# A two-layer decoder trunk on one core: three moves in the order of transposes, loads and sums

## The chip, the core and the metric

The kernel runs on one core of a Trainium2 chip. The metric is the time of one execution on the device in microseconds (us). Lower is better. The engines are TensorE (PE in the profile; PEld is its loading of weights), VectorE (DVE), ScalarE (ACT), GpSimd (POOL) and SyncE (SP), which issues nearly all DMAs in one queue.

## What is computed

The input x has 512 rows of 1024 float32 values. Two layers follow, each a token mixer and a gated MLP, every one ahead of a plain residual add. The first mixer is a gated DeltaNet, the second an attention with a sliding window whose keys and values are projected once. Cut to what the change touches:

```python
def gated_deltanet(hn, w_in, conv_w, a_log, dt_bias, out_norm_w, w_out):
    proj = hn @ w_in                      # q, k, v, z, b, a
    ...
    beta = sigmoid(b)
    g = -exp(a_log) * softplus(a + dt_bias)
    o = chunked_gated_delta_rule(q, k, v, g, beta)   # triangular inverse per chunk, then a scan over chunks
    o = rmsnorm(o, out_norm_w) * silu(z)
    return o.reshape(bsz, t, GDN_V_DIM) @ w_out

def shared_kv(h, kv_norm_w, w_kv):
    kv = rmsnorm(h, kv_norm_w) @ w_kv
    k, v = jnp.split(kv, 2, axis=-1)
```

The trunk is x + gated_deltanet, + conv_gated_mlp, then shared_kv, + sliding_window_sink_attention, + conv_gated_mlp, and a last rmsnorm.

## The kernel before

**Products in three passes.** Every large product is made of float32r matmuls of 128 x 512 in three passes (mm3): the high part of the weights by the high part of the data (L145), by its low part (L146), and the low part of the weights by the high part of the data (L147). Data lie with features on the partitions and the 512 tokens along the row, in pieces xh and xl of 128 features. A load of 1 MB brings 256 columns of a weight matrix into `stage` (two buffers). `cast` makes of each half of it a tile whi on ScalarE (L129) and a tile wlo on VectorE (L130), three buffers each. A product sums eight pieces, so 24 matmuls, into a PSUM bank. There are three banks d, two g, two s and one p.

**What sets the order.** Each engine works through its own list in order. A scheduler builds the lists from the program's text, from priorities and from its own costs. In the DeltaNet part a table of words (ORDER, with SHIFT) gives the priorities: key, query and value projections, z projections of the output gates ("z"), the inverses ("I"), their blocks ("L"), the scan ("C"), the gates ("g"). So whatever moves one step can move many others. SP's queue is one such list. A DMA that waits there holds back all that follow.

**The first part.** x is normalized and transposed, then the first key projection and the 48 gate columns are multiplied. The gate chain (L285 to L301) runs over ScalarE and VectorE: sigmoid, softplus, a scan over each chunk (L289) and the differences R (L292). R is transposed by L324 into a g bank and copied into `gt`, of which ngc, egc, egd and egl are made. `columns` (L185 to L196) loads a table of per-channel numbers into an `acc` row (L189), transposes it through a g bank (L192) and copies it out (L194). The MLP's conv table fcw comes in two such pieces. The key norms transpose kT (L385), also through g.

**The inverse and the scan.** For each group of four heads, `solve` (L511, L517) inverts the 32-wide diagonal blocks on VectorE. The result goes to DRAM (td, L520) and comes back as four loads into Xg (L523). `levels` then joins the blocks for each of two pairs of heads, in four dependent steps on PE: L541/L542 into s, copied to pz by ScalarE (L543, L544); L548 to L550 into s, negated by VectorE into Xg and sy (L552 to L554); L561 into p, copied to p6s by ScalarE (L564); L568 into s, subtracted by VectorE from sy (L571). After that come the four chunks of the scan: L588 with the state S, L603 with sy into s, copied to us (L607), L611 for the next state (L617), L628 for the output (L631). Between such dependent steps stand products of projections, which keep PE at work.

**Gates and residual.** `gate` loads a head's output (L667) and its z (L668), scales it by f_c, the output norms, on ScalarE (L671), transposes it (L674), multiplies it (L675) and stores it as yd (L676). The output projection loads yd back (L766), splits each row in a high and a low part (L150, L151) and makes mm3 products of it. YROLE names the buffers: heads 12 and 13 are ktok, 14 and 15 are vt. The residual is x transposed: for each of eight pieces a load into an `acc` row (role hsq, L777), four transposes into g (L780), a copy into h (L781).

**Keys and values.** `attention` normalizes h into kxh and kxl, calls `rstd_rows` and then loops over keys (kv = 0) and values (kv = 1), each with a load of 1 MB and two products. `rstd_rows` sums squares on ScalarE and VectorE (L797, L801), multiplies by ones (L804), takes the root (L806, L807), spreads it (L816, L823) and copies it (L825); the products are scaled by it (L1118), and keys are split into kbh and kbl (L1125 to L1128). The queries follow. Ahead of the attention lies the first MLP, `ffn(0, hT)`, whose last down products (L990 to L992) go straight over into the key products on PE.

Of the kernel before, what the change touches and what calls it, by code (L numbers as in the profile page):

```python
# [17 lines left out]
P = 128  # L18
T = 512
# [22 lines left out]
def kernel(  # L42
# [34 lines left out]
    def nm(s):  # L77
        cnt[0] += 1
        return f"{s}_{cnt[0]}"
# [30 lines left out]
    def bank(tag):  # L110
        return psum.tile([P, T], F32, tag=tag, bufs=BANKS[tag], name=nm(tag))

    def const(shape, dt=F32, s="c"):
        return cp.tile(list(shape), dt, name=nm(s))


    def load_stage(w, r0, kt, c0):
        st = wpool.tile([P, 8, 256], F32, tag="stage", bufs=2, name=nm("stage"))
        SP.dma_start(st[:, :kt, :], tiles_of(w, r0, kt, c0))
        return st  # L120
# [4 lines left out]
    def cast(st, kt, half, m=P):  # L125
        hi = wpool.tile([P, 8, P], F32R, tag="whi", bufs=3, name=nm("whi"))
        lo = wpool.tile([P, 8, P], F32R, tag="wlo", bufs=3, name=nm("wlo"))
        src = st[:, :kt, half * P : half * P + m]
        S.copy(hi[:, :kt, :m], src)  # L129
        V.tensor_tensor(lo[:, :kt, :m], src, hi[:, :kt, :m].bitcast(F32), op=ALU.subtract)  # L130
        return hi, lo

    def weights():
        return [wpool.tile([P, 8, P], F32R, tag=t, bufs=3, name=nm(t)) for t in ("whi", "wlo")]
# [184 lines left out]
    mnegr = const([P, P], F32R, s="mnegr")  # L319
    S.copy(mnegr[:], mneg[:])  # L320

    gtp = bank("g")
    for c in range(NC):
        PE.transpose(gtp[:, c * 80 : c * 80 + 80], R[0:80, c * P : (c + 1) * P], ident[0:80, 0:80])  # L324
    gt = const([P, NC, 80], s="gt")
    S.copy(gt[:], gtp[:, 0 : NC * 80].rearrange("p (c r) -> p c r", c=NC))

    def hc(ap):
        return ap.rearrange("p c h -> p h c")

    beta_t, gc_t, gd_t = hc(gt[:, :, 0:16]), hc(gt[:, :, 32:48]), hc(gt[:, :, 64:80])
    ngc = const([P, 16, NC], s="ngc")
    V.tensor_scalar(ngc[:], gc_t, -1.0, None, op0=ALU.mult)
    egc = const([P, 16, NC], s="egc")
    S.activation(egc[:], gc_t, AF.Exp)
    negegc = const([P, 16, NC], s="negegc")
    V.tensor_scalar(negegc[:], egc[:], -1.0, None, op0=ALU.mult)
    egd = const([P, 16, NC], s="egd")
    S.activation(egd[:], gd_t, AF.Exp)
    gl16 = const([P, 16, NC], s="gl16")  # L340
    V.tensor_tensor(gl16[:], gc_t, gd_t, op=ALU.add)
    egl = const([P, 16, NC], s="egl")
    S.activation(egl[:], gl16[:], AF.Exp)

    Xg = main.tile([P, 4, T], F32, tag="Xg", bufs=1, name="Xg")
    G.memset(Xg[:], 0.0)
# [407 lines left out]
    def r2(role, dt=F32):  # L754
        return row(nxt(role, ROLES[role]), dt)

    def wide(role):
        return pair(nxt("wide", YROLE), F32R)


    yh, yl = [], []
    for h2 in range(HV // 2):
# [8 lines left out]
    h22 = [pair("pz") for _ in range(2)]  # L771
    hT = [h4[:, m, :] for m in range(4)] + [h22[m // 2][:, m % 2, :] for m in range(4)]
    h_pairs = [h4[:, 0:2, :], h4[:, 2:4, :], h22[0][:], h22[1][:]]
    for m in range(KD):
        xr = r2("hsq")
        x3 = xr[:].rearrange("p (c e) -> p c e", c=NC)
        SP.dma_start(x3, x[0, :, m * P : (m + 1) * P].rearrange("(c p) e -> p c e", p=P))  # L777
        pt = bank("g")
        for c in range(NC):
            PE.transpose(pt[:, c * P : (c + 1) * P], x3[:, c, :], ident[:])  # L780
        S.copy(hT[m], pt[:])  # L781
# [11 lines left out]
    def rstd_cols(h):  # L793
# [16 lines left out]
    def third_stage():  # L810
        return main.tile([P, 6, 256], F32, tag="st3", bufs=1, name=nm("st3"))

    def rstd_rows(h):
        rt = rstd_cols(h)
# [287 lines left out]
    def attention(h):  # L1102
# [5 lines left out]
                G.memset(t[0:64, 1, :].bitcast(F32), 0.0)  # L1108
                G.memset(t[64:128, 0, :].bitcast(F32), 0.0)
        kxh, kxl = normed(h, NKV)  # L1110
        rs = rstd_rows(h)
        for kv in range(2):
            st = load_stage(w_kv, 0, 8, 256 * kv)
            for i in range(2):
                ps = bank("d")
                mm3(ps[:], cast(st, 8, i), KD, kxh, kxl)
                f = r2("va")
                V.tensor_tensor(f[:], ps[:], rs[:], op=ALU.mult)  # L1118
                if kv == 0:
                    for j in range(2):  # L1120
                        g = 2 * i + j
                        src = f[64 * j : 64 * j + 64, :]
                        near, far = (slice(0, 64), slice(64, 128)) if j == 0 else (slice(64, 128), slice(0, 64))
                        hn_, hf_ = kbh[g][near, j, :], kbh[g][far, 1 - j, :]
                        S.copy(hn_, src)  # L1125
                        S.copy(hf_, src)
                        V.tensor_tensor(kbl[g][near, j, :], src, hn_.bitcast(F32), op=ALU.subtract)
                        V.tensor_tensor(kbl[g][far, 1 - j, :], src, hn_.bitcast(F32), op=ALU.subtract)  # L1128
                else:
                    pt = bank("g")  # L1130
                    for c in range(NC):
                        PE.transpose(pt[:, c * P : (c + 1) * P], f[:, c * P : (c + 1) * P], ident[:])
                    S.copy(Vp[:, :, i * P : (i + 1) * P], pt[:].rearrange("p (c e) -> p c e", c=NC))
# [84 lines left out]
                V.tensor_tensor(h[m], h[m], ps[:], op=ALU.add)  # L1218

    ffn(0, hT)  # L1220
    attention(hT)
    ffn(1, hT, last=True)

# [52 lines left out]
```

## Time and profile before

| what | value |
|---|---|
| median of 3 runs | 1440.92 us (1440.52 to 1442.91) |
| the profiled execution | 1439.8 us, its span 1438.0, so 1.8 us lie outside the span |
| mean granted TensorE clock | 0.996 |
| PE idle in the span | 36.6 us, 8.2 of them while the first piece of x comes in |

The span is what the profiler saw from the first to the last instruction. A row of a timeline has the start, the duration, engine, line, operation, out<-in, the tile's size and, in brackets, how long the engine stood idle before it and whom it waited for. In a row of SP the duration is that of the issue, or, with a count, the stretch that several issues take. A row of waits has the total, the number and the longest. Matmuls of 128 x 512 show a duration of 0.39 us but start 0.23 us apart, because they are pipelined.

### The profile page before, as it was taken

To read this page: it belongs to the slowest core of one execution; us is meant where nothing else is said; L and a number is where in the kernel's file an instruction comes from. 1 tells how busy PE (TensorE), PEld (TensorE's weight loads), DVE (VectorE), ACT (ScalarE), POOL (GpSimd) and SP (SyncE) were. 2 spreads that over 40 slices of the span, in tenths; PEclk is the share of its full clock that TensorE was granted. 3 is DMA by queue.
4 is the path that set the end of the run, shared out by engine and by line. 5 is a ranking of instruction groups with operands and counts; after the bars stand their busy time and mean duration, and the time that the engine had idled before them with its cause. 6 is when DMAs were issued, how large, how long until landed. Compare 5 with 4: busy or idle time off the path is not lost.

```text
span 1438.0 us, 21635 instructions
## 1 busy us (share of the span) xinstructions
PE 1401.4 (97%) x8266; PEld 1165.2 (81%) x8266; DVE 1120.6 (78%) x2056; ACT 770.8 (54%) x1518; POOL 20.0 (1%) x47
## 2 busy tenths in 40 slices
PE   7999999999999999999999999999999999999998
PEld 5777878878876888888988888777788888988887
DVE  5896887979764538889968889787757888977896
ACT  7764666666555434444335445588745444344443
POOL 1000000000000000000000002000000000000000
PEclk9999999999999999999999999999999999999999
DMA  5334254264367323321333223311132322332222
GB/s 156 88 106 114 78 174 121 76 182 125 103 220 227 125 88 110 104 74 53 123 124 111 74 81 111 111 59 45 59 108 90 118 81 66 112 123 88 96 70 77
DMA packets 163084, 152.85 MB, mean 106 GB/s; under 512 B 24164, under 2 KB 150693, under 8 KB 162981
## 3 DMA queue, kind: packets, MB, share of 16 engines
q1 hardware_dynamic: 160722, 151.27, 33.3%
q8 instruction: 65, 1.06, 0.3%
q10 hardware_dynamic: 2259, 0.20, 0.2%
q14 instruction: 38, 0.31, 0.1%
HBM read 134.65 MB, written 16.80 MB: 105 GB/s over the span
## 4 chain that ended last, share of the span: by engine, by line
PE 83%; DVE 8%; DMA 6%; ACT 2%; issue 1%; SPq 0%; DVEq 0%; ACTq 0%
PE d L145 21%; PE d L147 20%; PE d L146 20%; DVE wlo L130 2%; PE s L588 1%; PE p L1191 1%; DMA ol<-od 1%; PE d L992 1%; PE g L1186 1%; PE s L603 1%; PE s L628 1%; PE d L990 1%; PE s L992 1%; PE d L991 1%; DMA stage<-in_a_w_in_dram 1%
## 5 line engine op out<-in xcount | busy, mean ns | idle before, releaser
L145 PE MATMUL d<-xh,whi 128*128 128x512 f32 x1192 | 475.2, 400 | 2.9 <-ACT whi L129 2.8
L146 PE MATMUL d<-xl,whi 128*128 128x512 f32 x1192 | 472.8, 398 | 0.0
L147 PE MATMUL d<-xh,wlo 128*128 128x512 f32 x1192 | 472.0, 398 | 0.7 <-DVE wlo L130 0.7
L129 ACT CAST whi<-stage 128x1024 fp32r<-128x1024 f32 (+2 forms) x236 | 229.1, 976 | 230.3 <-PE d L146 153.9
L130 DVE TENSOR_TENSOR wlo<-stage,whi 128x1024 fp32r<-128x1024 f32 (+2 forms) x236 | 265.5, 1129 | 69.2 <-ACT whi L129 68.6
L145 PEld LDWEIGHTS d<-xh,whi 128*128 128x128 f32 x1192 | 224.6, 188 | 51.2 <-ACT whi L129 3.4
L147 PEld LDWEIGHTS d<-xh,wlo 128*128 128x128 f32 x1192 | 224.3, 188 | 51.5 <-DVE wlo L130 2.1
L146 PEld LDWEIGHTS d<-xl,whi 128*128 128x128 f32 x1192 | 224.3, 188 | 46.2 <-issue 1.0
L237 DVE SCALAR_TENSOR_TENSOR acc<-d,cwc,acc 128x511 f32<-128x511 f32 (+2 forms) x96 | 70.7, 739 | 8.3 <-ACT acc L234 7.9
L851 DVE TENSOR_TENSOR sz<-d,p6s 128x512 f32<-128x512 f32 x58 | 39.9, 689 | 40.9 <-PE d L147 38.4
L873 ACT ACTIVATE dt<-dt 128x512 f32<-128x512 f32 x44 | 27.8, 632 | 81.7 <-DVE dt L856 81.7
L856 DVE SCALAR_TENSOR_TENSOR va<-sz,fcw,va 128x511 f32<-128x511 f32 (+1 forms) x58 | 43.4, 747 | 1.8 <-ACT va L854 0.9
L856 DVE SCALAR_TENSOR_TENSOR dt<-sz,fcw,dt 128x511 f32<-128x511 f32 (+1 forms) x58 | 43.3, 746 | 0.9
L511 DVE TENSOR_TENSOR p6s<-sN,sT 64x31 f32<-64x31 f32 (+15 forms) x124 | 40.7, 328 | 2.5 <-DMA sN<-nd 0.5
L517 DVE TENSOR_TENSOR sT<-sT,p6s 64x31 f32<-64x31 f32 (+15 forms) x124 | 41.0, 330 | 1.9
L129 ACT CAST whi<-st 128x768 fp32r<-128x768 f32 (+1 forms) x30 | 23.7, 791 | 30.5 <-DMA st<-in_ffn_w_down_dram 5.6
L851 DVE TENSOR_TENSOR zl<-d,p6s 128x512 f32<-128x512 f32 x30 | 20.7, 689 | 24.0 <-PE d L147 23.3
L636 ACT ACTIVATE rq<-o 128x128 f32<-128x128 f32 x64 | 19.0, 298 | 28.4 <-DVE o L631 15.8
L1174 ACT ACTIVATE dt<-dt,sm 128x256 f32<-128x256 f32 (+1 forms) x64 | 30.3, 474 | 6.7 <-DVE sm L1170 6.6
L875 DVE TENSOR_TENSOR va<-dt,va 128x512 f32<-128x512 f32 x44 | 30.4, 691 | 1.2
L130 DVE TENSOR_TENSOR wlo<-st,whi 128x768 fp32r<-128x768 f32 (+1 forms) x30 | 26.8, 898 | 1.9 <-ACT whi L129 1.8
L854 ACT ACTIVATE dt<-sz,normc,fcw 128x512 f32<-128x512 f32 x29 | 23.7, 817 | 5.2 <-DVE sz L851 5.1
(745 smaller groups left out, 2796.5 us busy)
## 6 DMA issues: line engine op xcount, KB each, us to landing
stage<-in_ffn_w_up_dram SPq DMA_DIRECT2D x44, 1024.0 KB, 5.2
stage<-in_a_w_in_dram SPq DMA_DIRECT2D x23, 1024.0 KB, 5.8
stage<-in_ffn_w_down_dram SPq DMA_DIRECT2D x16, 768.0 KB, 4.7
stage<-in_a_w_out_dram SPq DMA_DIRECT2D x8, 1024.0 KB, 5.5
st<-in_ffn_w_down_dram SPq DMA_DIRECT2D x8, 768.0 KB, 5.8
zd<-sz SPq DMA_DIRECT2D x16, 256.0 KB, 2.0
od<-o SPq DMA_DIRECT2D x16, 256.0 KB, 2.5
stage<-in_b_w_q_dram SPq DMA_DIRECT2D x4, 1024.0 KB, 5.0
```

The lines of the kernel that those rows point to most:

```text
L129: S.copy(hi[:, :kt, :m], src)
L130: V.tensor_tensor(lo[:, :kt, :m], src, hi[:, :kt, :m].bitcast(F32), op=ALU.subtract)
L145: PE.matmul(ps, hi[:, k, :m], xh[k], start=first and k == 0, stop=False)
L146: PE.matmul(ps, hi[:, k, :m], xl[k][:], start=False, stop=False)
L147: PE.matmul(ps, lo[:, k, :m], xh[k], start=False, stop=last and k == kt - 1)
L237: V.scalar_tensor_tensor(acc[:, d:], ps[:, : T - d], col, acc[:, d:], op0=ALU.mult, op1=ALU.add)
L511: V.tensor_tensor(tv, N[:, s, s + 1 : 32].unsqueeze(2).to_broadcast([64, n, m]), Tm[:, s : s + 1, 0:m].to_broadcast([64, n, m]), op=ALU.mult,)
L517: V.tensor_tensor(Tm[:, s + 1 : 32, 0:m], Tm[:, s + 1 : 32, 0:m], tv, op=ALU.subtract)
L851: V.tensor_tensor(u[:], ps[:], rs[:], op=ALU.mult)
L856: V.scalar_tensor_tensor(acc[:, d:], u[:, : T - d], tap(2 - d, t), acc[:, d:], op0=ALU.mult, op1=ALU.add)
L875: V.tensor_tensor(b[:], a[:], b[:], op=ALU.mult)
L1174: S.activation(e3[:, j, :], e3[:, j, :], AF.Exp, bias=ngm[:, j : j + 1], accum_out=den[:, j : j + 1])
```

## The change

It has three parts. The first wraps the gates' transposes and the six steps made of them in `tc.high_priority(-112000)`, which lowers their place in the table's order by 112 words. The second gives the residual's eight pieces of x rows of their own: three `f` rows, three pieces of the 6 x 256 buffer st3, and two more `f` rows. Six small GpSimd copies of f_c's column of head 8 into these rows set the time from which they may be filled. The third loads the key weights of w_kv into three `f` rows and the `gr` row after the first MLP's text (`load_rows`), where they are free in that MLP's second half, casts them from there in pieces of 128 x 256 (`cast_rows`), loads only the values through `stage`, and puts `rstd_rows` behind the keys' two products. New lines shift the numbers: L145 is L158 after, L192 is L205, L324 is L342, L385 is L400, L541 to L571 are L556 to L586, L603 is L618, L667 is L682, L777 and L780 are L801 and L804.

```diff
+    def load_rows(w, tags):
+        rows = [row(t)[:].rearrange("p (k c) -> p k c", k=2) for t in tags]
+        for i, r in enumerate(rows):
+            SP.dma_start(r, tiles_of(w, 2 * i * P, 2, 0))
+        return rows
+
+    def cast_rows(rows, half):
+        w = weights()
+        for i, r in enumerate(rows):
+            cast_to(w, 2 * i, r[:, :, half * P : half * P + P])
+        return w
...
-    gtp = bank("g")
-    for c in range(NC):
-        PE.transpose(gtp[:, c * 80 : c * 80 + 80], R[0:80, c * P : (c + 1) * P], ident[0:80, 0:80])
-    gt = const([P, NC, 80], s="gt")
...
+    with tc.high_priority(-1000 * 112):
+        gtp = bank("g")
+        for c in range(NC):
+            PE.transpose(gtp[:, c * 80 : c * 80 + 80], R[0:80, c * P : (c + 1) * P], ident[0:80, 0:80])
+        gt = const([P, NC, 80], s="gt")
...
+    x6 = third_stage()[:].rearrange("p k c -> p (k c)")
+    xrows = [row("f")[:] for _ in range(3)] + [x6[:, T * u : T * u + T] for u in range(3)]
+    for xr in xrows:
+        G.tensor_copy(xr[:, 0:1], f_c[:, 8, 0:1])
+    xrows += [row("f")[:] for _ in range(2)]
     for m in range(KD):
-        xr = r2("hsq")
-        x3 = xr[:].rearrange("p (c e) -> p c e", c=NC)
+        x3 = xrows[m].rearrange("p (c e) -> p c e", c=NC)
...
-        rs = rstd_rows(h)
         for kv in range(2):
-            st = load_stage(w_kv, 0, 8, 256 * kv)
+            if kv == 1:
+                st = load_stage(w_kv, 0, 8, 256 * kv)
+            products = []
             for i in range(2):
                 ps = bank("d")
-                mm3(ps[:], cast(st, 8, i), KD, kxh, kxl)
+                mm3(ps[:], cast(st, 8, i) if kv else cast_rows(key_weights, i), KD, kxh, kxl)
+                products.append(ps)
+
+            if kv == 0:
+                rs = rstd_rows(h)
+            for i, ps in enumerate(products):
                 f = r2("va")
...
     ffn(0, hT)
+    key_weights = load_rows(w_kv, ("f", "f", "f", "gr"))
     attention(hT)
```

The scheduler builds new lists from this. Three places follow, as the lists give them. The first is PE's list around the gates, before and after: d_121 and d_131 are products of key and query projections, g_69 is the gates' bank, g_88, g_91 and g_94 are those of `columns`, g_103 the key norms'. Before:

```order
L146 MATMUL d_121_541<-xl_45_196,whi_122_542 128x512
L324 MATMUL g_69_322<-ident_6_80,sz_60_280 128x80
L192 MATMUL g_88_363<-ident_6_80,acc_87_358 128x17
L147 MATMUL d_121_541<-xh_44_195,wlo_123_543 128x512
L324 MATMUL g_69_322<-ident_6_80,sz_60_280 128x80 x2
L145 MATMUL d_131_632<-xh_23_132,whi_132_633 128x512
L324 MATMUL g_69_322<-ident_6_80,sz_60_280 128x80
L192 MATMUL g_91_369<-ident_6_80,acc_90_367 128x128
```

After:

```order
L160 MATMUL d_131_632<-xh_44_195,wlo_133_634 128x512
L342 MATMUL g_69_322<-ident_6_80,sz_60_280 128x80
L205 MATMUL g_88_363<-ident_6_80,acc_87_358 128x17
L342 MATMUL g_69_322<-ident_6_80,sz_60_280 128x80 x3
L205 MATMUL g_91_369<-ident_6_80,acc_90_367 128x128
L205 MATMUL g_94_375<-ident_6_80,acc_93_373 128x128
L400 MATMUL g_103_418<-kT_49_205 128x128 x4
L158 MATMUL d_135_667<-xh_23_132,whi_136_668 128x512
```

The gates moved behind all 24 products of d_131, and the columns' transposes with them. Before, fourteen matmuls stand between g_91's transpose and g_94's; after, none does.

The second is SP's queue when the last group's inverse comes back from DRAM (td to Xg), with the gates' loads (ol, zl), z's stores (zd) and gate stores (yd). Before:

```order
L520 DMA td_354<-sT_549_3446 64x1024
L523 DMA Xg_341<-td_354 32x16x32 x2
L676 DMA yd_357<-zl_624_4072 128x512
L667 DMA ol_626_4086<-od_355 128x4x128
L523 DMA Xg_341<-td_354 32x16x32
L668 DMA zl_627_4087<-zd_356 128x512
L523 DMA Xg_341<-td_354 32x16x32
L667 DMA ol_629_4101<-od_355 128x4x128
```

After (the six loads of x by L801 stand some rows ahead of it):

```order
L675 DMA zd_356<-sz_674_4319 128x512
L538 DMA Xg_341<-td_354 32x16x32
L683 DMA zl_627_4087<-zd_356 128x512
L683 DMA va_676_4323<-zd_356 128x512
L682 DMA ol_629_4101<-od_355 128x4x128
L538 DMA Xg_341<-td_354 32x16x32
L691 DMA yd_357<-zl_627_4087 128x512
L538 DMA Xg_341<-td_354 32x16x32
L682 DMA ol_632_4116<-od_355 128x4x128
L683 DMA zl_630_4102<-zd_356 128x512
L538 DMA Xg_341<-td_354 32x16x32
```

The second to fourth loads of Xg moved behind the loads of gates 9 to 11 and the store of gate 9.

The third is PE's list at the same group's second pair of heads: s_620 is its second step, p_621 and s_622 the third and fourth, s_635 the first product of the scan, d_687 a z projection. Before:

```order
L550 MATMUL s_620_4020<-sy_618_3999,pz_78_344 32x32
L146 MATMUL d_687_4403<-xl_27_142,whi_688_4404 128x512
L147 MATMUL d_687_4403<-xh_26_141,wlo_689_4405 128x512
L145 MATMUL d_687_4403<-xh_29_150,whi_688_4404 128x512
L561 MATMUL p_621_4048<-Xg_341,nt_543_3416 64x64 x8
L146 MATMUL d_687_4403<-xl_30_151,whi_688_4404 128x512
L147 MATMUL d_687_4403<-xh_29_150,wlo_689_4405 128x512
L145 MATMUL d_687_4403<-xh_32_159,whi_688_4404 128x512
L568 MATMUL s_622_4059<-sy_618_3999,p6s_79_345 64x64 x8
L603 MATMUL s_635_4131<-vt_589_3771,sy_613_3927 128x128 x2
```

After:

```order
L565 MATMUL s_620_4020<-sy_618_3999,pz_78_344 32x32
L576 MATMUL p_621_4048<-Xg_341,nt_543_3416 64x64 x8
L583 MATMUL s_622_4059<-sy_618_3999,p6s_79_345 64x64
L618 MATMUL s_635_4131<-vt_589_3771,sy_613_3927 128x128
L583 MATMUL s_622_4059<-sy_618_3999,p6s_79_345 64x64 x7
L618 MATMUL s_635_4131<-vt_589_3771,sy_613_3927 128x128
```

The z products between the steps moved ahead of the whole pair; the last of them stand between the second and third step of the first pair (s_615 and p_616).

More of the change, by code (lines that the diff above doesn't have):

```diff
@@ L758, in wide, with third_stage @@
         return pair(nxt("wide", YROLE), F32R)
+    def third_stage():
+        return main.tile([P, 6, 256], F32, tag="st3", bufs=1, name=nm("st3"))
     yh, yl = [], []
@@ L808, in rstd_cols @@
         return rt
-    def third_stage():
-        return main.tile([P, 6, 256], F32, tag="st3", bufs=1, name=nm("st3"))
     def rstd_rows(h):
```

28 lines of the change are left out of this document (14 added, 14 removed).

## The prediction

> **What bounds the kernel now.** I read the page first, then TensorE's waits, then the granted clock of the stretches around the longest waits. The page's second line gives the bound:
>
> ```profile
> PE 1401.4 (97%) x8266; PEld 1165.2 (81%) x8266; DVE 1120.6 (78%) x2056; ACT 770.8 (54%) x1518; POOL 20.0 (1%) x47
> ```
>
> TensorE is busy 1401.4 us, 97% of the span, so only the 3% in which it isn't, and what the clock loses behind them, can be won. The waits say where they lie (line, what was waited for, total, times, longest):
>
> ```profile
> PE d L145 <- ACT whi L129: 2.8, 1, 2.8
> PE g L324 <- DVE sz L292: 2.4, 1, 2.4
> ...
> PE g L780 <- DMA acc<-in_x_dram: 1.6, 3, 0.7
> ...
> PE s L588 <- DVE S L617: 1.0, 1, 1.0
> PE g L385 <- ACT kT L238: 0.9, 1, 0.9
> PE g L780 <- DVE va L675: 0.8, 1, 0.8
> ...
> PE g L1132 <- DVE va L1118: 0.7, 1, 0.7
> ```
>
> The change aims at five of them: L324 (the gates), both of L780 (the residual), L145 with its 2.8 and L1132 (keys and values). The stretches (busy us of PE, PEld, DVE, ACT and POOL, then the granted clock) show what follows a long wait:
>
> ```profile
> 37.00:40.00 3.00, 0.57 (x4) 0.18 (x2) 2.90 (x10) 0.66 (x2) 0.00 (x0) 1.00 0.44 93
> 40.00:44.00 4.00, 4.00 (x14) 3.17 (x14) 2.70 (x6) 3.93 (x5) 0.00 (x0) 0.57 0.63 213
> 400.00:420.00 20.00, 20.00 (x256) 15.99 (x254) 9.23 (x19) 9.75 (x28) 0.61 (x2) 1.00 0.60 197
> 890.00:897.00 7.00, 4.23 (x31) 3.71 (x30) 7.00 (x13) 4.91 (x6) 6.50 (x13) 1.00 0.45 151
> 897.00:905.00 8.00, 7.79 (x29) 5.82 (x28) 6.25 (x8) 3.42 (x6) 0.18 (x1) 0.79 0.40 132
> ```
>
> After 2.4 us without work the clock is 0.57 for 4 us, which loses 4 x 0.43 = 1.7 us more; after 2.8 us it is 0.79 for 8 us (8 x 0.21 = 1.7). The row 400 to 420 is full: that stretch has nothing to win, and it matters below.
>
> **Part A, the gates.** The rows around the wait (start, duration, engine, line; behind them a load and its time from issue to landing):
>
> ```profile
> 36.70 0.39 PE L145 MATMUL d<-xh,whi 128*128 128x512 f32 x1
> 36.93 0.40 PE L146 MATMUL d<-xl,whi 128*128 128x512 f32 x1
> 39.75 0.26 PE L324 MATMUL g<-ident,sz 80*128 80x80 f32 x1 [2.43 <-DVE sz L292]
> ...
> 43.77 0.42 PE L145 MATMUL d<-xh,whi 128*128 128x512 f32 x1
> ```
> ```profile
> 37.43 0.37 SPq L119 DMA_DIRECT2D stage<-in_a_w_in_dram  x1
> 40.22 0.34 SPq L189 DMA_DIRECT2D acc<-in_ffn_conv_w_dram  x1
> ```
> ```profile
> acc<-in_ffn_conv_w_dram SPq DMA_DIRECT2D x1, 64.0 KB, 2.9
> ```
> ```profile
> stage<-in_a_w_in_dram SPq DMA_DIRECT2D x23, 1024.0 KB, 5.8
> ```
>
> A product starts 0.23 us behind the one ahead of it. From 37.16 (36.93 + 0.23) to 43.77, 6.6 us, PE did some 2.4 us of work, seven products and six small transposes: the gates' place costs 4.2 us now. In the new order 25 products run there, so PE is at the gates at 37.16 + 25 x 0.23 = 42.9, when the VectorE chain (done at 39.75) has long ended: that wait goes.
>
> But the columns' transposes and the key norms (L385, now L400) keep their turn behind the gates on the two g banks, so they move too, and with them a load. The second conv table (acc_93) takes the row of acc_87, which is free only when g_88 is transposed, after the gates: about 43.4, not 40.2. SP's queue now has the next 1 MB of weights (stage_215) just ahead of it, which needs only wlo_146 and is issued at about 43. Behind the gates PE has one more transpose (g_91) and then stands at g_94 with everything queued behind it, all products of the next key and query projections included. If the table lands 2.9 us after its issue as before, at 46.3, the wait is about 2.6 us; if behind the 1 MB, at 43 + 5.8 = 48.8, about 5. Either ends in the slow clock again (1.7). So 4.3 to 6.7 in place of 4.2, less the 0.9 that the key norms wait now: -0.8 to +1.6.
>
> Which end? The table issued at 40.22 landed at 43.1; the 1 MB ahead of it, issued at 37.43, at 37.43 + 5.8 = 43.2 by the median. They landed together. I take **+1.3**, near the upper end.
>
> The Trainium skill says the same of a queue (DMA: Bandwidth & Descriptors, "Queues, rings and completion order": on each DMA engine a queue's descriptors are consumed in ring order). By that the small load moves last, at 48.8, and part A is +1.6; this trace agrees as far as one pair of loads can.
>
> **Part B, the residual.** Its columns of x now go to eight rows of their own, so both waits of L780 (1.6 + 0.8 = 2.4) end. The six POOL copies that time the loads stand beside an idle engine: nothing. What I look at is the order that comes with them. SP's blocks of the inverse (Xg) fall behind gate loads:
>
> ```profile
> 391.11 0.42 SPq L523 DMA_DIRECT2D Xg<-td  x1
> ...
> 399.98 0.53 SPq L667 DMA_DIRECT2D ol<-od  x1
> ```
>
> The fourth block goes out at 391.11 now. In the new queue it stands behind the ol load that goes out at 399.98 now and waits for gate 10's transposes, so it lands about 9 us later. PE doesn't wait for that, since 29 products of the last z projections are put ahead of the first step instead. Those products, however, are what covers the later steps today (the full row 400 to 420). In the new order the last step of the first pair and all of the second pair's stand bare: each waits for a copy or a subtraction on another engine.
>
> ```profile
> 395.12 0.36 ACT L543 COPY pz<-s 32x256 f32<-32x256 f32 x1
> 395.49 0.37 ACT L544 COPY pz<-s 32x256 f32<-32x256 f32 x1
> ```
> ```profile
> 400.42 0.42 DVE L552 TENSOR_SCALAR Xg<-s 32x256 f32<-32x256 f32 x1 [1.13 <-PE s L550]
> ```
> ```profile
> 401.93 0.76 ACT L564 COPY p6s<-p 64x256 f32<-64x256 f32 x2 [3.02 <-PE p L561]
> ```
> ```profile
> 403.45 0.85 DVE L571 TENSOR_TENSOR sy<-sy,s 64x256 f32<-64x256 f32 x2 [1.74 <-PE s L568]
> ```
> ```profile
> 411.75 0.59 ACT L607 COPY us<-s 128x512 f32<-128x512 f32 x1 [0.98 <-PE s L603]
> ```
> ```profile
> 424.13 0.68 DVE L151 TENSOR_TENSOR qT<-sz,kT 128x512 fp32r<-128x512 f32 x1
> ```
>
> With 0.1 us from one engine to the next: s_617 behind p_616 0.8 (0.76 + 0.1, little beside it), s_620 behind s_619 0.8 (0.36 + 0.37 + 0.1), p_621 behind s_620 0.5 (0.42 + 0.1), s_622 behind p_621 0.9, s_635 behind s_622 0.7 (0.85 + 0.1 and a split of 0.68 that stands ahead on VectorE, less four products of 0.23), p_637 behind s_635 0.25 (0.59 + 0.1 less two products). That is **+4.0**, from 0 (the waits of the scan behind it take them up) to +5. The scan gets some of the cover: of its 1.0 (L588) I take 0.8 back, between 0 and 1.0. The last gates' products (ktok, vt) come from the chain that now starts later, while the x transposes that lay between are done early: I give back 1.2 of the 2.4, between 0 and 3. Sum: 4.0 - 0.8 - 2.4 + 1.2 = **+2.0**, ends -3.4 and +5.6.
>
> **Part C, the keys.**
>
> ```profile
> 896.73 0.50 PE L145 MATMUL d<-xh,whi 128*128 128x512 f32 x1 [2.77 <-ACT whi L129]
> ```
> ```profile
> 877.06 13.68 SPq L119 DMA_DIRECT2D stage<-in_w_kv_dram  x2
> ```
> ```profile
> 889.93 0.42 DVE L140 TENSOR_TENSOR wlo<-stage,whi 128x256 fp32r<-128x256 f32 x1
> ```
>
> The SP row holds both loads of w_kv, the keys' at 877.06 and the values' at its end, 890.7, when a slot came free; that is why the first value product waits 2.77. With the keys in f and gr rows the values take the slot of 877 and are there. What lies here is 2.8, the 1.7 of the clock behind it, and L1132's 0.7: 5.2. What is late next: whi of that product, an estimated 0.2, because eight short casts (L139 and L140 in form) stand where two long ones stood; wlo of the keys, whose second piece of 0.42 stands behind two xl on a VectorE that is full there (7.00 of 7), 0.5; and at the end va and the key splits (L1132 again), whose rs is ready no earlier than now, 0.8. The sums of squares, moved behind the keys' products, are the same instructions on VectorE and its queue holds the key casts ahead of them; rs is needed only at the products' end. Gain 5.2 - 1.5 = **-3.7**. If the products wait for whole tiles and not pieces (seven more pieces of 0.42 behind the first, 2.9), it is -0.8; with no wait left, -5.2.
>
> **The sum.** -3.7 + 1.3 + 2.0 = -0.4 against the profiled execution's 1439.8, so 1439.4 on its basis; the median of the runs, 1440.92, lies 1.1 above it, so 1440.5 there. 0.2% is 2.9 us: faster is under 1438.0, slower over 1443.8.
>
> **The rivals.** *Forecast, no change*, 0.36: 1438 to 1443.
> *Slower: the clock falls in the bare steps.* Point: from the wait of s_617 on, PE is idle for about 4 of 10 us. If the activity there is too thin to hold the clock, 10 x 0.43 = 4.3 us come on top: 1440.5 + 4.3 = 1444.8. For it: 0.57 after one wait of 2.4. Against it: no single wait here reaches 1 us. 0.14. The Trainium skill (TensorE: Matmul & The Clock Gate, Part 1) has the clock drop only after a whole window of about 3.4 us without enough work; by that it would not fall for gaps under 1 us, though no row here shows such a series.
> *Faster: the cover isn't missed.* The solve's chain is a chain either way, and the scan waited 1.0 us with it; if bare steps only move those waits and the last gates find fewer, part B is -2.0: 1440.5 - 4.0 = 1436.5. For it: PE's work is the same, and products not spent in these steps are left for the scan (32 in place of 29). Against it: the steps are short and PE is in order. 0.25.
> *The table lands in its own 2.9 us.* Part A -0.8: 1440.5 - 2.1 = 1438.4. Against it: the pair that landed together. 0.14.
> *The key casts are the new bound.* VectorE is full in 890 to 897; with whole tiles waited for, part C is -0.8: 1440.5 + 2.9 = 1443.4. Against it: the products behind the two-piece casts of L139 and L140 start today between the pieces. 0.11.
>
> Faster: 0.24 of the third, 0.05 of the fourth, 0.03 of the forecast: 0.32. Slower: 0.12, 0.04 and 0.02: 0.18. The rest, 0.5, is no change. The range runs from the faster rival with a little more (1435.5) to the slower one (1444.8).
>
> **What would show it.** A: no wait at the gates, and a new one of 2.6 to 5 us on the columns' transpose behind an acc load, with the clock low after it. B: no wait on x columns; in the last steps of `levels` five waits of 0.5 to 0.9, and the row that was 20.00 of 20 near 400 to 420 under 17. C: no whi wait over 0.5 near 894 and a full clock behind it. I am wrong if these steps show no waits (then 1436.5 or less) or if the last gates' products wait over 3 us.

## The result and the profile after

The changed kernel takes **1452.45 us** (median of 4 runs, 1452.3 to 1453.98) beside 1441.28 us for the kernel before on the same chip: ratio 1.0078, 95% interval 1.0061 to 1.0096. It is 11 us slower, where the forecast was no change (1440.5, range 1435.5 to 1444.8). The profiled execution has a span of 1450.7 us, 12.7 more than before's (whose profiled execution was a quick one, 1439.8). Ratios, here and below, leave out two executions at a granted clock of 0.655 and 0.753 (1971 us, of before, and 1719 us, of e3). Of the three parts one did what was forecast (the keys), one did nothing (the residual), and one lost 13 us (the gates), most of it at places where the change edits nothing.

The waits of TensorE in the kernel after (total, times, longest), to be held against the same view of before; the row left out at the top is the start of the kernel:

```profile
...
PE g L205 <- DMA acc<-in_ffn_conv_w_dram: 5.6, 1, 5.6
...
PE g L689 <- ACT ol L686: 3.2, 4, 2.0
PE g L505 <- ACT va L251: 2.8, 2, 1.8
PE g L689 <- ACT dt L686: 2.0, 1, 2.0
...
```

The waits of before at the gates (2.4), at the x columns (1.6 and 0.8) and at the key weights' whi (2.8) are gone. In their place stand one at the second conv table, and several at steps that the change doesn't touch: transposes of gates (L689) and values (L505) and, in rows further down, the steps of an inverse (L583, L563, L576).

**Where the 12.7 us went.** Waits alone don't add up to them, because the clock falls behind some. So I gave each matmul its median spacing in the trace of before (0.229 us for 512 columns of 128 rows, 0.118 for 256, 0.111 for 128, and so on), which makes 1340.9 us in every kernel, and read at what time each kernel had issued the same sum. The table gives, in us, how far each kernel fell behind before in each stretch of before's time. The first column is the start-up, which changes from execution to execution. A trace is one execution and not the median: those of e2, e12 and e14 are the slowest of their runs, those of e1 and e7 the fastest, so an end can differ by some us from what the medians say (e2: 3.5 here, and no change over its ten runs). The runs e1 to e14 are told below; e9 to e11 have no row.

| kernel | to 30 | 30–75 | 75–200 | 200–300 | 300–405 | 405–425 | 425–800 | 800–950 | rest | end |
|---|---|---|---|---|---|---|---|---|---|---|
| after | 0.9 | **4.9** | 1.2 | **3.0** | **2.4** | **4.4** | -0.9 | **-3.3** | -0.1 | 12.6 |
| e1 gates alone | 1.5 | 4.0 | 0.9 | 3.2 | -0.9 | 6.1 | -1.7 | -0.2 | 0.0 | 12.9 |
| e2 residual alone | 1.0 | 0.1 | 0.2 | 0.5 | 0.5 | 0.4 | 0.4 | 0.4 | 0.2 | 3.5 |
| e3 keys alone | 0.3 | 0.1 | 0.3 | 0.4 | 0.0 | 0.0 | 0.5 | **-3.5** | 0.9 | -1.0 |
| e4 residual and keys | 0.7 | 1.4 | 0.4 | 0.3 | 0.6 | 0.4 | -0.2 | -3.6 | 0.3 | 0.3 |
| e5 tables late | 1.2 | 9.0 | 1.7 | 4.4 | 0.8 | 6.2 | -1.9 | 0.0 | -0.2 | 21.0 |
| e6 tables' own rows | 2.2 | 1.1 | 2.1 | 5.5 | 1.8 | 0.9 | -1.2 | -1.4 | -0.4 | 10.5 |
| e7 gates, own rows | 0.9 | -0.5 | 1.4 | -0.9 | 0.1 | 5.6 | 0.4 | -0.3 | 0.2 | 7.1 |
| e8 gates by 105 | 1.1 | 6.2 | 1.6 | -0.8 | 2.7 | 1.3 | 0.5 | -0.7 | -0.1 | 11.8 |
| e12 gates, lists kept | 1.0 | **-4.4** | **21.4** | -0.6 | 0.2 | **0.0** | 0.4 | 1.2 | 0.0 | 19.4 |
| e13 gates, V later | 1.0 | -0.4 | 5.1 | -0.5 | 1.7 | 1.0 | 5.1 | -0.5 | 0.1 | 12.6 |
| e14 gates, z earlier | 1.1 | 0.5 | 5.4 | 1.4 | 0.3 | 0.9 | 2.7 | -0.1 | -0.1 | 12.3 |

**The table of the second conv** (30 to 75). The queue of SP, TensorE's row at the columns, and the stretches (busy us of PE, PEld, DVE, ACT, POOL, then the granted clock) in the kernel after:

```profile
38.62 5.89 SPq L119 DMA_DIRECT2D stage<-in_a_w_in_dram  x2
44.69 0.45 SPq L202 DMA_DIRECT2D acc<-in_ffn_conv_w_dram  x1
```
```profile
50.38 0.45 PE L205 MATMUL g<-ident,acc 128*128 128x128 f32 x1 [5.58 <-DMA acc<-in_ffn_conv_w_dram]
```
```profile
44.80:50.30 5.50, 0.00 (x0) 0.00 (x0) 3.15 (x6) 3.11 (x6) 0.00 (x0) 0.78 0.68 206
50.30:55.00 4.70, 4.62 (x16) 4.13 (x17) 2.75 (x5) 3.07 (x4) 0.00 (x0) 0.53 0.00 0
```

The 1 MB goes out just ahead of the 64 KB table (the second issue of the first row ends at 44.51). The table is there 5.7 us after its issue. It took 2.9 before, where it went out 2.8 us behind a load of 1 MB (40.22 and 37.43). TensorE does nothing for 5.6 us and then works at 0.53 for 4.7 us, which loses 2.2 more.

**Values** (near 280). VectorE's and TensorE's rows:

```profile
277.78 0.73 DVE L250 SCALAR_TENSOR_TENSOR acc<-d,cwc,acc 128x509 f32<-128x509 f32 x1
278.44 0.40 DVE L526 TENSOR_TENSOR p6s<-sN,sT 64x255 f32<-64x255 f32 x1
```
```profile
282.73 0.66 PE L505 MATMUL g<-ident,va 128*128 128x128 f32 x4 [1.75 <-ACT va L251]
```

The three conv steps of a value head stand between steps of the diagonal inverse, one by one, and TensorE's list asks for the transposed values at once. In before the same steps alternate too, but its list spreads the transposes, and none waits. TensorE's rows of these transposes with their places in the list (va, the first three value heads of one group), before and then after:

```order
1120 L490 MATMUL g_438_2738<-ident_6_80,va_431_2699 128x128 x4
1131 L490 MATMUL g_444_2783<-ident_6_80,va_439_2747 128x128 x4
1150 L490 MATMUL g_452_2831<-ident_6_80,va_445_2792 128x128 x4
```
```order
1128 L505 MATMUL g_438_2738<-ident_6_80,va_431_2699 128x128 x4
1131 L505 MATMUL g_444_2783<-ident_6_80,va_439_2747 128x128 x4
1132 L505 MATMUL g_452_2831<-ident_6_80,va_445_2792 128x128 x4
```

Ten and eighteen rows stand between them before; two and none after.

**Gate outputs** (near 313). SP's, ScalarE's and TensorE's rows in the kernel after:

```profile
303.66 0.38 SPq L119 DMA_DIRECT2D stage<-in_a_w_in_dram  x1
...
306.98 0.53 SPq L682 DMA_DIRECT2D ol<-od  x1
```
```profile
313.27 1.28 ACT L686 ACTIVATE ol<-ol,fc 128x128 f32<-128x128 f32 x4 [3.74 <-DMA ol<-od]
```
```profile
313.73 0.33 PE L689 MATMUL g<-ident,ol 128*128 128x128 f32 x1 [1.97 <-ACT ol L686]
```

The ol load goes out 3.3 us behind a 1 MB load, and TensorE waits for what comes of it. The list alone doesn't make this loss. The gates' part by itself (e1) has the same rows here and sends the load as far behind the same 1 MB (303.16), but has it 4.1 us later and not 6.3, and TensorE doesn't wait:

```profile
306.47 0.53 SPq L669 DMA_DIRECT2D ol<-od  x1
```
```profile
310.56 1.28 ACT L673 ACTIVATE ol<-ol,fc 128x128 f32<-128x128 f32 x4 [1.53 <-DMA ol<-od]
```

**The bare steps** (420 to 436). TensorE's rows, then the stretches:

```profile
423.53 0.32 PE L583 MATMUL s<-sy,p6s 64*64 64x64 f32 x2 [0.47 <-ACT p6s L579]
426.04 0.21 PE L563 MATMUL s<-pz,sy 32*32 32x32 f32 x1 [0.84 <-ACT pz L559]
427.26 1.12 PE L576 MATMUL p<-Xg,nt 64*64 64x64 f32 x16 [0.53 <-DVE Xg L567]
428.91 0.47 PE L583 MATMUL s<-sy,p6s 64*64 64x64 f32 x2 [0.52 <-ACT p6s L579]
```
```profile
423.32:426.73 3.41, 2.37 (x96) 1.97 (x96) 1.59 (x3) 1.97 (x5) 0.16 (x1) 1.00 0.74 271
426.73:433.56 6.83, 5.78 (x42) 4.74 (x42) 5.52 (x9) 3.24 (x6) 0.30 (x1) 0.50 0.49 157
```

In the last inverse four waits of 0.5 to 0.8 stand as foretold, and the clock falls with them, to 0.50 for 6.83 us, though no wait is longer than 0.84.

**Keys** (800 to 950): the only wait left at the key products, and the stretch around it.

```profile
912.10 0.50 PE L160 MATMUL d<-xh,wlo 128*128 128x512 f32 x1 [0.20 <-DVE wlo L153]
```
```profile
908.00:912.00 4.00, 3.78 (x18) 2.42 (x17) 3.89 (x9) 2.73 (x5) 3.67 (x8) 1.00 0.65 227
```

No wait for whi, and a full clock.

### The profile page after: what moved, and what is told of

It is laid out like the page before. It is cut to its first block, busy times and chain, and to the rows that moved or that the text cites. A ratio compares the mean times of both kernels' runs of the same rounds, so it can differ in the third digit from the quotient of the medians.

```text
span 1450.7 us, 21665 instructions
## 1 busy us (share of the span) xinstructions
PE 1407.4 (97%) x8266; PEld 1171.1 (81%) x8266; DVE 1120.4 (77%) x2062; ACT 772.3 (53%) x1525; POOL 21.2 (1%) x53
## 4 chain that ended last, share of the span: by engine, by line
PE 84%; DVE 7%; DMA 6%; ACT 2%; issue 1%; SPq 0%; DVEq 0%; ACTq 0%
PE d L159 20%; PE d L158 20%; PE d L160 20%; DVE wlo L130 2%; DMA ol<-od 2%; PE s L603 2%; PE p L1218 1%; PE d L1013 1%; PE s L618 1%; PE g L1213 1%; PE s L643 1%; PE s L1013 1%; PE d L1011 1%; PE d L1012 1%; PE s L1011 1%
## 5 line engine op out<-in xcount | busy, mean ns | idle before, releaser
L158 PE MATMUL d<-xh,whi 128*128 128x512 f32 x1192 | 474.9, 399 | 1.0 <-DVE acc L250 0.7
L158 PEld LDWEIGHTS d<-xh,whi 128*128 128x128 f32 x1192 | 224.7, 189 | 51.6 <-issue 1.9
```

Source lines behind the costliest of these rows:

```text
L158: PE.matmul(ps, hi[:, k, :m], xh[k], start=first and k == 0, stop=False)
```

## The experiments

Theory R is the prediction's: the residual's loads cause the bare steps, and the gates' part costs little. The first rival, theory G, puts the whole loss on the gates' part. What came after separates, within the gates' part, the wait for the table (theory W) from the lists that the scheduler deals anew (theory L).

### The parts one by one: e1 to e4

Each is the kernel before with one part of the diff of the change (e4 with two).

> The gates' part alone. Theory G (the gates' move re-deals the lists of the whole first layer, and all the losses come from it): about +16 us, 1457, with the wait of 5 to 6 us on the second conv table, the waits on value and gate transposes near 280 and 313 and the bare steps of the last inverse all there. Theory R (the prediction's: the gates cost 1 to 2 us and the bare steps come from the residual's loads): 1442 to 1443, and the last inverse is covered as before.

Measured: 1454.88 us, ratio 1.0106 (1.0085 to 1.0127). TensorE's rows at the second conv table and in the last inverse of the gates' part alone:

```profile
50.34 0.45 PE L192 MATMUL g<-ident,acc 128*128 128x128 f32 x1 [4.95 <-DMA acc<-in_ffn_conv_w_dram]
423.25 0.26 PE L550 MATMUL s<-pz,sy 32*32 32x32 f32 x1 [0.83 <-ACT pz L546]
```

The gates' part alone has the table's wait, the waits near 280 and the bare steps. It has no wait near 313, where G had one too.

> The residual's part alone. Theory G: about -2 us, 1439, the waits on x columns gone, the last inverse covered, the residual's waits 0 to 1 us. Theory R: +2 us, 1443, with five waits of 0.5 to 0.9 in the last inverse.

Measured: 1440.8 us, ratio 0.9996 (0.9986 to 1.0005). The last inverse stays covered; x's transposes wait all the same, the longest time for something else:

```profile
459.36 0.63 PE L787 MATMUL g<-ident,f 128*128 128x128 f32 x4 [2.68 <-DVE va L675]
...
467.28 0.63 PE L787 MATMUL g<-ident,f 128*128 128x128 f32 x4 [1.02 <-DMA f<-in_x_dram]
```
```profile
458.46 0.75 DVE L675 SCALAR_TENSOR_TENSOR va<-g,onwc,va 128x512 f32<-128x512 f32 x1 [4.70 <-DMA va<-zd]
```

With the data there, the g bank isn't: a gate's transposes hold it until z is back from memory and multiplied in (L675). The second wait is still for x itself, in a row that is filled late. The 2 us that G had as a gain don't come either.

> The key weights' part alone, rstd_rows behind the keys' products included. Both theories: -3.7 us, 1437.5, the whi wait near 894 gone and the clock full behind it.

Measured: 1438.88 us, ratio 0.9975 (0.9964 to 0.9986), faster. What is left at the key products is a wait of 0.29 for wlo.

> Residual and keys together, the gates left where they were. Theory G: -5.5 us, 1435.5. Theory R: -1.7 us, 1439.5.

Measured: 1439.33 us, ratio 0.9986 (0.9976 to 0.9995). On where the loss comes from, theory R falls and G holds: without the gates' part nothing is lost, and with it alone as much as in the whole change. G's amounts missed, since e4 gains 2 us and not 5.5. That R's 1439.5 for e4 came out is luck: neither its bare steps nor its gain at the x columns is there.

### The wait or the lists: e5 to e8

e5 leaves the gates alone and only lowers the two conv tables in the order:

```diff
-    fcw = [columns([fconv_rows[l, 0:128, :]], 128, "fcw") for l in range(2)]
+    with tc.high_priority(-1000 * 300):
+        fcw = [columns([fconv_rows[l, 0:128, :]], 128, "fcw") for l in range(2)]
```

> The gates and everything else keep their text; only the two conv tables of the MLPs (fcw) get a lower priority (300 words), so that their transposes stand 24 products later. Their loads keep their place in SP's queue, so no product should wait for a table; the wait of 2.4 at the gates stays. But the lists behind are dealt anew much as with the gates' part: in the last inverse no product of a projection stands between the steps. Theory W (the loss of the gates' part starts with the 5.6 us for the second table and what is pushed back by it): as before, 1441, within 2 us. Theory L (the lists of the first layer, dealt anew, cost 8 us by themselves: transposes that wait for silu and for loads near 280 and 310, bare steps near 415): 4 to 9 us slower, with the same waits near 415 as in the changed kernel.

Measured: 1461.12 us, ratio 1.0145 (1.013 to 1.016), the slowest of all. No product waits for a table's load. Rows of TensorE at a conv sum, at the values and in the last inverse:

```profile
56.39 0.77 PE L145 MATMUL d<-xh,whi 128*128 128x512 f32 x1 [3.77 <-DVE acc L237]
...
287.81 1.11 PE L490 MATMUL g<-ident,va 128*128 128x128 f32 x4 [1.75 <-ACT va L238]
...
431.78 0.25 PE L548 MATMUL s<-pz,sy 32*32 32x32 f32 x1 [0.84 <-ACT pz L544]
```

The losses at the values and at the bare steps come with the gates in their old place and no wait for a table. W falls for these; L had them right, and was too low at the conv sums.

e6 is the kernel before with a row of its own for each conv table, and e7 the same with the gates' part:

```diff
-        st = row("acc", n=P)
+        st = row("acc", n=P) if s != "fcw" else const([P, P], s="fct")
```

> The kernel before with a row of its own for each of the two conv tables, so that they are loaded at the start and no transpose can wait for them. The gates keep their place. The lists are dealt anew, but the last inverse keeps two or three products between its later steps. W: no wait removed (the tables were no wait before), so as before, within 2 us. L: as before or by whatever the new lists do, minus 3 to plus 3 us; no bare steps near 415.

Measured: 1452.94 us (1445.08 to 1456.03), ratio 1.008 (1.0053 to 1.0107). Both theories missed: a change that takes nothing away from anybody costs 12 us. In the trace, which lies 10.5 behind, about half of it is lost at the values:

```profile
283.34 1.11 PE L490 MATMUL g<-ident,va 128*128 128x128 f32 x4 [1.75 <-ACT va L238]
```

> The gates' part with a row of its own for each conv table: the wait of 5 us for the second table must go, and so must the slow clock behind it. By W the gates' move then shows its gain: 3 to 4 us faster than before. By L it loses only some 5 of its 13 us: 4 to 9 us slower than before, because the list of the last inverse has no products between its steps from the end of its first pair on.

Measured: 1449.45 us, ratio 1.0061 (1.0043 to 1.0079). TensorE at the first conv table and in the bare steps:

```profile
46.91 0.33 PE L192 MATMUL g<-ident,fct 128*128 128x128 f32 x1 [1.88 <-DVE onwc L194]
...
414.44 0.26 PE L548 MATMUL s<-pz,sy 32*32 32x32 f32 x1 [0.84 <-ACT pz L544]
```

With the table's wait gone the kernel is level with before until 405 us, and then loses 5.6 in the bare steps. So L's amount was right, and its place; W is out.

e8 has the gates' part with a shift of 105 in place of 112:

```diff
+    with tc.high_priority(-1000 * 105):
```

> The gates' part with a shift of 105 words in place of 112. The gates' transposes hardly move (the last of the four goes behind the transpose of the first conv table), the second table's load stays ahead of the 1 MB load, so the waits of 2.4 at the gates stay and the wait of 5 at the table should not come. The lists behind are dealt anew (1472 rows of TensorE's list differ from before), with the steps of the last inverse covered. W: as before within 2 us. L: as before or by whatever the new lists do, minus 3 to plus 3 us, and clearly less than with 112.

Measured: 1451.59 us, ratio 1.0077 (1.0062 to 1.0092): no better than with 112, and both theories missed. The gates' transposes trade one place with a table's, and the comparison of TensorE's list with before's still has 1472 lines. (Such a comparison also counts the unchanged lines that it prints round each difference; here and below the counts are for holding kernels against each other.) VectorE and TensorE then:

```profile
59.99 0.69 DVE L429 TENSOR_TENSOR dt<-dt,brk 128x512 f32<-128x512 f32 x1 [3.37 <-ACT dt L427]
...
65.06 4.02 DVE L237 SCALAR_TENSOR_TENSOR acc<-d,cwc,acc 128x511 f32<-128x511 f32 x6
```
```profile
68.57 0.47 PE L145 MATMUL d<-xh,whi 128*128 128x512 f32 x1 [3.19 <-DVE acc L237]
```

The conv steps of the query heads now stand behind the decays (dt), for which VectorE waits 3.4 us; TensorE waits for the bank that they hold. By the lists alone, without a run, a shift of 100 gives a comparison of 8 lines, and from 101 on 1472 to 1714. L in its simple form (the covered list is harmless) falls with e6 and e8: each new deal has a price of its own, at places of its own.

### The residual's bank: e9, e10

Residual and keys, with x transposed through other banks (e10 "p" in place of "s"):

```diff
-        pt = bank("g")
+        pt = bank("s")
```

> The residual's and the keys' parts without the gates' part, and the transposes of x go through the s banks in place of the g banks, so that they don't stand behind the last gates' transposes, whose bank is held until z is back from memory. Theory B (the residual's gain was lost to that bank): the wait of 2.2 to 2.7 us of an x transpose on a gate's multiply goes, and the kernel is 2 to 3 us faster than residual and keys with g banks (ratio 0.9986), so about 5 faster than before. Rival Z (PE only comes sooner to the next thing that waits for the last z or output to come back, the gate transposes or the first output products): the wait moves behind the x transposes, and the time stays at 2 us faster than before, within 1.

Measured: 1438.09 us, ratio 0.9982 (0.9968 to 0.9995).

```profile
460.67 1.14 PE L157 MATMUL d<-ktok,whi 128*128 128x512 f32 x2 [1.94 <-ACT ktok L162]
```

> The same with the transposes of x through the single p bank, which the scan's last steps use too. Theory B: as with the s banks, 5 us faster than before, less some tenths where one bank has to be copied out between two transposes. Rival Z: 2 us faster than before, with a wait on the last gates or on the first products with their values.

Measured: 1439.99 us, ratio 0.9993 (0.9982 to 1.0003), with a wait of 2.4 for vt and one of 1.4 for ktok. Rival Z holds: the x transposes no longer wait for a gate, and the products with the last gates' values (ktok, vt) wait in their place.

### The keys without the moved sums: e11

The keys' part, with `rstd_rows` ahead of the key products as before (the lines are held against e3):

```diff
+        rs = rstd_rows(h)
         for kv in range(2):
...
-            if kv == 0:
-                rs = rstd_rows(h)
```

> The keys' part without its last move: the key weights are loaded ahead and cast in pieces, but the sums of squares stay ahead of the products in the program, so that VectorE has their six additions between the key casts. The prediction's view (the load carries the gain, the move of the sums only keeps VectorE's queue short): the whi wait of 2.8 is gone all the same, the low casts come up to 1.5 us later; 2 to 3 us faster than before where the whole part has 3.6. Rival (the move of the sums carries it): no faster than before, since the products wait 3 us for the low casts.

Measured: 1440.12 us, ratio 0.9997 (0.9988 to 1.0007): no gain.

```profile
897.63 0.51 PE L159 MATMUL d<-xh,wlo 128*128 128x512 f32 x1 [2.28 <-DVE wlo L152]
```

The rival holds. With the six additions of squares between the low casts the wait for the load turns into one for wlo. The moved load is worth nothing without the moved sums; the sums without the load weren't run.

### The gates with the lists of before: e12 to e14

e12 has the gates' part, own rows (e6) and late tables (e5). Its lists differ from before up to some 115 us and then come back to them (a comparison of 325 lines on TensorE, where the gates' part alone has 1714).

> The gates' part, and the two conv tables have rows of their own and a priority lower by 300 words. The gates stand where the change puts them, but the lists come back to those of before after about 110 us (325 rows of TensorE's list differ, where the gates' part alone has 1714). The transposes of the first group (key norms, values, decays) are crowded behind the tables near 100 us, so a few waits there are likely. Theory L (the later losses come from the lists): the gates' wait goes, no loss at 275 to 320 and none near 415, where the lists are those of before; what is left is minus 2 to minus 4 at the gates and plus 1 to plus 5 near 100 us, so 3 us faster to 2 slower than before. Theory D (whatever reaches those places later or sooner than the list was made for loses there, with the same list too): new waits at 275 to 320 and 415 all the same, 5 us or more slower.

Measured: 1457.32 us, ratio 1.0114 (1.0099 to 1.0129). TensorE's rows behind the late tables, and the stretches there and at the three places where the other kernels lose:

```profile
80.81 0.80 PE L416 MATMUL g<-gr,skr 128*128 128x512 f32 x1 [3.51 <-ACT dt L427]
...
86.23 1.12 PE L490 MATMUL g<-ident,va 128*128 128x128 f32 x4 [3.18 <-ACT dt L427]
```
```profile
76.00:95.00 19.00, 10.47 (x39) 7.07 (x38) 12.62 (x25) 17.36 (x41) 0.00 (x0) 0.64 0.29 78
270.00:300.00 30.00, 30.00 (x154) 25.02 (x154) 28.42 (x67) 21.00 (x58) 0.00 (x0) 1.00 0.20 63
300.00:330.00 30.00, 29.66 (x219) 23.32 (x217) 23.68 (x45) 15.27 (x33) 0.00 (x0) 1.00 0.69 202
405.00:440.00 35.00, 34.03 (x374) 26.91 (x372) 17.64 (x31) 18.53 (x48) 0.61 (x2) 1.00 0.60 186
```

Three things are told apart here. The gates' move itself gains 4.4 us by 75 (the forecast had 4.2 for what their old place costs). The first group's small products, crowded behind the tables, lose 21, of which I had expected 1 to 5, so L's time is missed by far. And from 200 to 800 us, 18 us late but with the lists of before, it loses nothing: rows all but full, a full clock. Theory D falls, though the time is in its range. The losses of the other kernels near 280 and in the bare steps come with their lists and not with being late.

e13 and e14 are e7 with one more word shifted (in e14 `'z': -1` stands in place of `'V': 1`):

```diff
-SHIFT = {"R": 6, "B": -28, "g": -40, "K": -1, "N": 7, "C": -2, "P": -3}
+SHIFT = {'R': 6, 'B': -28, 'g': -40, 'K': -1, 'N': 7, 'C': -2, 'P': -3, 'V': 1}
```

> The gates' part with own rows for the tables (1449.45, of whose loss the lag in the trace puts 7.5 us at the bare steps near 415) and the value projections one word later in the table (SHIFT V: 1). In the lists so dealt the gates stand as in the change and the steps of the last inverse have two or three products between them again. If the bare steps are the loss: no waits near 415 and 4 to 8 us better than 1449.45, 1441.5 to 1445.5. Rival (each new deal loses somewhere, the bare steps are only one of the places): 1446 or more, with other waits, at the conv sums near 65, at the value transposes near 280 or at the gate transposes.

Measured: 1451.41 us, ratio 1.0078 (1.0055 to 1.0102).

```profile
187.87 0.33 PE L490 MATMUL g<-ident,va 128*128 128x128 f32 x1 [2.30 <-ACT va L238]
...
468.38 1.09 PE L780 MATMUL g<-ident,acc 128*128 128x128 f32 x4 [5.00 <-DVE va L675]
```

> The same with the z projections one word earlier in place of the value projections later (SHIFT z: -1). Again the steps of the last inverse are covered and the gates stand as in the change. If the bare steps are the loss: 1441.5 to 1445.5. Rival: 1446 or more, with waits at other places than in the run beside it.

Measured: 1448.81 us (1445.28 to 1452.07), ratio 1.0045 (1.0025 to 1.0064), with the same wait of 2.30 at the value transposes of the second group.

With cover the stretch of the bare steps costs 0.9 to 1.0 and not 5.6, as intended (the expectation's 7.5 is more than the table gives e7 for this stretch), and the rival holds all the same: both lose 5 at the values of another group, and e13 5 more near the x transposes. That e14 would wait at other places than e13 was wrong.

The fastest version by its ratio is the keys' part alone (e3, 3.6 us faster than before; the interval of e9 overlaps with its own). No kernel that moves the gates or the tables is as fast as before.

## Why the prediction was wrong, point by point

**Part A (+1.3 forecast).** The mechanism stood: no wait at the gates, the table behind the 1 MB, the slow clock after it. What the old place cost was put at 4.2, and e12 gains 4.4; 1.7 of it is a slow clock that not every execution has (last section). The size of the new cost was off: 4.3 to 6.7 forecast, 5.6 + 2.2 = 7.8 measured, so +3.6 where I took +1.3 with 1.6 as the end (the table shows 4.9 by 75, a wait of 0.7 at a conv sum included). A reading was wrong as well: the 0.9 taken off for the key norms is no wait behind the gates. It stands at another group, 160 us later:

```profile
206.51 1.16 PE L385 MATMUL g<-kT 128*128 128x128 f32 x8 [0.91 <-ACT kT L238]
```

Without it the same sum gives +2.2, between +0.1 and +2.5. The rival in which the table lands in its own 2.9 us is out: 5.7. By the Trainium skill (DMA: Bandwidth & Descriptors, "Queues, rings and completion order") part A was +1.6; the rows agree with the order in the ring, but the cost began later and lasted longer than I had worked out.

**The step that failed** is one that the prediction took without a word: that moving the gates changes TensorE's work near them and no more. The sum has no term for anything else, and the part that it puts at +1.3 costs 13 by itself (e1). I compared the lists of the whole change with those of before, read the bare steps off them rightly, and put them down to part B, because B is near them in the text. They come from part A: e1 has them, e2 does not. And I looked only at the places that I already knew from before's waits; the value transposes near 280 stood in the same lists. They cost 3.0 of the 12.7 us and the bare steps 4.4; e1 has both (3.2 and 6.1). The 2.4 between 300 and 405 are not part of this step as far as the runs show: e1, with the same rows, doesn't lose them.

**Part B (+2.0 forecast).** The residual's part is worth nothing measurable (e2). Of the forecast's terms, -2.4 for x's waits happened, and 2.68 (a gate's bank) and 1.0 (x in a late row) came in their place in e2, a wait of 2.0 for a gate's dt in the whole change: the "late ktok, vt" term was right in kind (e9, e10 show it bare), and larger than the 1.2 that I took. The 4.0 for the bare steps isn't B's. As a price for bare steps it was right by accident: the four waits are 2.4 in sum, and with the clock the stretch loses 4.4. The 0.1 us that the sum takes from one engine to the next stands in no row; in the kernel after, ScalarE's va (`282.03 0.65 ACT L251`) ends 0.05 before the transposes that wait for it start. So the rival "the clock falls in the bare steps", to which I gave 0.14, is what happened there, at lower waits than I had reckoned with.

**Part C (-3.7 forecast).** Measured -3.3 in the whole change, -3.5 and -3.6 in e3 and e4. The whi wait and the slow clock behind it are gone, wlo waits 0.2 to 0.3. I had given the load all the credit and the move of the sums none; by e11 the load alone gains nothing.

**What stays open.** Where each of the nine kernels that move the gates or the tables lost its 6 to 21 us is shown place by place in their traces, but not why the list of before has none of these waits. Why the ol load near 313 took longer in the whole change than in e1 isn't shown. That its words and shifts were chosen with that list is likely and wasn't tried. Nor was a list found that keeps the 4.4 us of the gates.

## What to carry to other kernels

Where a scheduler deals the lists, a move has two prices: its own, and that of the new deal. Build each part of a change by itself and compare its lists with those of before on all engines; if they differ in hundreds of rows behind the place of the edit, the local sum says little (in e12 the 4.4 us won at the gates came with 21 lost behind them). And when a wait is to be removed, name what holds the same engine next, the bank, the cast or the value that comes last, since a moved load alone was worth nothing in two of the three parts.

## What the runs showed of the hardware

The granted clock in these traces is full or half, and it changes only at steps of 3.41 us; values between, such as 0.53, 0.57 or 0.79, are mixes of the two. It falls without any long wait. Ahead of the bare steps' 6.83 us at half clock TensorE was busy for 2.37 of 3.41 us, with products of 32 x 32 and 64 x 64, and no wait was over 0.84. In e1, e5 and e7 the half clock lasted 10.24 us there, and the same stretch cost 5.6 to 6.2 where it cost 4.4 in the kernel after. In e12 it was half for 13.65 us from 78 on and for 6.83 from 95 on, with waits of up to 3.5. The Trainium skill (TensorE: Matmul & The Clock Gate, Part 1) has the clock drop after an idle window of about 3.4 us; the length agrees with these traces, but TensorE wasn't idle throughout the window in any of the cases named here, and the measurement decides.

The share of idle time alone doesn't decide. In e8 TensorE was busy for less, 1.79 of 3.41 us, with products of 128 rows, and the clock stayed full:

```profile
366.32:369.73 3.41, 1.79 (x10) 1.15 (x9) 2.29 (x6) 2.64 (x11) 0.00 (x0) 1.00 0.08 29
369.73:373.15 3.42, 3.42 (x26) 3.03 (x25) 2.66 (x6) 1.30 (x4) 0.00 (x0) 1.00 0.02 5
```

So the small products seem to count for less than the time that they are busy; no run varies them alone.

What a wait costs in clock depends on where it falls. The gates' wait of 2.4 to 2.7 us is followed by half clock for 3.41 us in before, e2, e3 and e11, for 6.83 in e4 and e10, and in e9, where a step falls into the middle of a wait of 2.62, by none:

```profile
37.54:47.78 10.24, 7.62 (x42) 6.05 (x41) 8.04 (x19) 6.69 (x12) 0.00 (x0) 1.00 0.47 129
```

The 1.7 us that the prediction puts behind such a wait is therefore what one execution had, and not a fixed price.

A 64 KB load that took 2.9 us, sent 2.8 us behind a load of 1 MB, takes 5.7 right behind one in the same queue, which agrees with the ring order that the Trainium skill gives (DMA: Bandwidth & Descriptors, "Queues, rings and completion order").
